# A two-layer Gated DeltaNet and GLA trunk: the scheduler orders the same instructions by its timeline simulation

## The chip, the core and the metric

The kernel runs on 1 core of a Trainium2 chip. The metric is device time in microseconds (us) of one execution, the median of several runs. The engines are PE (TensorE, with PEld its weight loads), DVE (VectorE), ACT (ScalarE), POOL (GpSimd) and SP (SyncE, which only issues DMAs here). Each engine takes its instructions from a queue of its own in the order that the built program gives it, and waits on semaphores for work of the others.

## The reference

One sequence of 2048 tokens with 1024 channels, float32, through two layers. Layer 0 mixes tokens by a gated delta rule (8 heads, keys of 128, values of 256), layer 1 by gated linear attention (GLA, 4 heads). Each layer ends in an output projection, a residual and a layer norm.

```python
def gdn_mixer(x, w_in, conv_w, a_log, dt_bias, norm_w, w_out):
    p = x @ w_in
    qkv = causal_conv_silu(p[..., :GDN_QKV], conv_w)
    ...
    beta = jax.nn.sigmoid(b_logit)
    g = -jnp.exp(a_log) * jax.nn.softplus(a_logit + dt_bias)
    o = gated_delta_rule(q, k, v, g, beta)   # q, k l2-normalised per head
    o = gated_rmsnorm(o, norm_w, gate)
    return o.reshape(B, T, GDN_VAL) @ w_out
...
    # gated_delta_rule, per chunk: (A + I) is unit lower triangular
    uw = triangular_solve(A + eye, rhs)
    def step(S, inp):
        v_new = u_n - w_n @ S
        o = qd_n @ S + qk_n @ v_new
        S = S * gl_n + kd_n.T @ v_new
...
def reference(x, ...):
    for i in range(DEPTH):       # 2: gdn_mixer, then gla_mixer
        x = layer_norm(DEEP_ALPHA * x + mixer(x), ln_g[i], ln_b[i])
```

## The kernel before, in words

The tokens are cut into 4 groups of 512, each of 4 chunks of 128. A *unit* is one head of one layer on one group: 32 DeltaNet units and 16 GLA units, 48 in all. PHASES sets the order of the groups: (layer 0, group 0), (0, 1), (1, 0), (0, 2), (1, 1), (0, 3), (1, 2), (1, 3), with all heads of a group one after the other.

Projections are done in float32r with high and low parts, three matmuls for each product (`mm3`, tiles `xh`, `xl`, `wc`); the recurrences are in float32. Four Python generators write the program (`plan.run`, line 931):

- `gemms` (line 432) writes the input projections of a unit: key and query (`kq`), value (`vt`) and gate (`sg`). They use 3 PSUM buffers `psg`. Weight tiles `wc` are streamed by SP through 16 buffers.
- `preps` (758), by `gdn_prep` (574): transposes of keys and queries, the masked products of keys and queries (`psc<-kq`), and the inverse of the unit triangular matrix of each chunk. For the 16x16 blocks on its diagonal, DVE masks the product (tile `W2`) and reduces it to `X`; ACT's queue issues a DMA of `X` to DRAM (`blk`), SP's queue one that reads it back repeated over partitions (`Arep`); then DVE does 15 steps of two small operations each, `Xt` and `X`. After that come matmuls with `U`, `W2` and `Tm`.
- `chains` (823), by `gdn_chain` (785): the recurrence over the 4 chunks of a unit. PE multiplies the state by the keys (`psh<-S,kq`), DVE makes `Rt`, PE multiplies it by the inverse (`psh<-Rt,D1`, where the inverse `Uf` has taken the tile `D1`), ACT copies the result to `wt`, PE does `psh<-wt,kd`, and DVE updates the state `S`. Beside it `psc<-S,qd` and `psc<-wt,D2` give the output, which DVE gates into `og`. `psh` has one buffer: the next use of it has to wait for DVE's update of `S`, the next head's first one too. At the end of the unit `og` is transposed (`psc<-cst,og`) and split into `oth` (ACT) and `otl` (DVE); the norm factor `z` is computed from `ms` by small DVE operations.
- `outs` (856): the output projection of the unit before, 8 blocks of 6 matmuls (`pso<-wo,oth` and `pso<-wo,otl`, one PSUM buffer), each added to the residual `y` by DVE.

```python
        for q in range(15, 0, -1):                                      # gdn_prep
            v.tensor_tensor(xt[:, :, :q], R[:, q, :, :q], X[:, :, q:q + 1].broadcast_to([P, NC, q]), ALU.mult)
            v.tensor_tensor(X[:, :, :q], X[:, :, :q], xt[:, :, :q], ALU.subtract)
...
            mm(d, p["kd"][:, n], wt[:])                                 # gdn_chain
            v.scalar_tensor_tensor(S[:], S[:], eg[:, 1, u.h, n:n + 1], d, ALU.mult, ALU.add)
```

A small planner in the kernel (`Plan`) keeps a rough clock with a cost for each operation. Each generator yields the time at which its next matmul could have its inputs, and the planner goes on with one that is due, so the four streams are interleaved as they are written. All operations pass through one helper, `Planned`, so every row of the profile has line 121, and rows are told apart by the names of tiles. The framework (`tile.TileContext`) then sets the final order of each engine's queue, allots the buffers and puts in the semaphores. Before the change its scheduler does that in its default way.

## Time and profile before

| | before |
|---|---|
| time, median of 3 runs | 3249.08 us (3248.84 to 3249.32) |
| the profiled execution | 3242.97 us |
| its span, first to last instruction | 3241.1 us |
| mean granted TensorE clock | 0.978 |
| busy: PE, PEld, DVE, ACT, POOL | 95%, 80%, 68%, 36%, 12% |
| DMA | 551.93 MB, mean 170 GB/s |

The profiled execution is one run of its own; its span is what the rows of the trace add up to. In rows of the timeline a row has the start in us from the span's start, the duration in us, the engine, the line, the operation with its tiles (out<-in), the shape, a count where equal instructions follow each other, and in brackets the idle time of the engine before it with what ended that. An fp32 matmul shows as two records. Buffer numbers are left out of the names there (`D` is D1 or D2, `S` the state of any head).

### The profile page before, as it was taken

What the parts mean: (1) busy time and instruction counts of PE and PEld (TensorE: products, weight loads), DVE (VectorE), ACT (ScalarE), POOL (GpSimd) and SP (SyncE); (2) the same over time, 40 slices, a digit from 0 to 9 for tenths busy, and PEclk for the clock granted to TensorE, in tenths of its full rate; (3) what the DMA queues carried; (4) which work ended last, traced back from release to release, by engine and by line L of the source; (5) the groups of instructions that cost most, each with busy time, mean ns of one, the idle gap of its engine ahead of it and who ended that gap; (6) DMA issues with size and microseconds to landing.
All of it is one profiled execution on the core that took longest, in us unless ns stands there. A gap on an engine that the chain in (4) does not pass through costs nothing. (4 is left out here: it accounts for less than half of the span.)

```text
span 3241.1 us, 52660 instructions
## 1 busy us (share of the span) xinstructions
PE 3064.3 (95%) x18430; PEld 2608.5 (80%) x18430; DVE 2192.7 (68%) x6201; ACT 1182.7 (36%) x3091; POOL 395.3 (12%) x642
## 2 busy tenths in 40 slices
PE   8889999998999998999999999999999999999997
PEld 6677777777887887887888788888787888888895
DVE  5776677686666757667767665756876665755677
ACT  4444443332232445433332334423332223343331
POOL 4422321020000223200100000100100000000011
PEclk9999999999999999999999999999999999999998
DMA  7876655464444556755544453655644445465453
GB/s 231 251 225 194 195 168 184 149 215 134 143 141 130 178 174 199 255 183 172 187 149 133 134 168 118 218 179 154 194 141 146 145 143 156 134 211 178 134 166 104
DMA packets 442489, 551.93 MB, mean 170 GB/s; under 512 B 37568, under 2 KB 381888, under 8 KB 430192
## 3 DMA queue, kind: packets, MB, share of 16 engines
q1 hardware_dynamic: 412656, 505.57, 50.3%
q10 hardware_dynamic: 29568, 43.00, 4.0%
q8 instruction: 145, 2.38, 0.3%
q14 instruction: 120, 0.98, 0.1%
HBM read 421.24 MB, written 127.21 MB: 169 GB/s over the span
## 5 line engine op out<-in xcount | busy, mean ns | idle before, releaser
L121 PE MATMUL psg<-xh,wc 128*128 128x512 f32 x2560 | 892.7, 408 | 6.2 <-ACT wc L121 3.2
L121 PE MATMUL psg<-wc,xh 128*128 128x256 f32 (+1 forms) x4096 | 795.8, 291 | 10.1 <-DVE sg L121 3.6
L121 PEld LDWEIGHTS psg<-wc,xh 128*128 128x128 f32 x4096 | 657.7, 191 | 38.9 <-DVE sg L121 4.0
L121 PEld LDWEIGHTS psg<-xh,wc 128*128 128x128 f32 x2560 | 488.8, 192 | 118.4 <-ACT wc L121 4.8
L121 PE MATMUL psg<-wc,xl 128*128 128x256 f32 (+1 forms) x2048 | 582.5, 285 | 0.0
L121 PE MATMUL pso<-wo,oth 128*128 128x512 f32 x1472 | 514.4, 427 | 30.4 <-DVE y L121 27.2
L121 PE MATMUL psg<-xl,wc 128*128 128x512 f32 x1280 | 519.5, 406 | 0.5 <-DVE xl L121 0.5
L121 DVE SCALAR_TENSOR_TENSOR y<-pso,z,y 128x512 f32<-128x512 f32 x368 | 274.4, 746 | 189.6 <-PE pso L121 175.5
L121 PEld LDWEIGHTS psg<-wc,xl 128*128 128x128 f32 x2048 | 391.4, 191 | 1.0
L121 DVE SCALAR_TENSOR_TENSOR acc<-pb,taps,acc 128x512 f32<-128x512 f32 x384 | 300.9, 785 | 116.9 <-ACT acc L121 112.0
L121 PE MATMUL pso<-wo,otl 128*128 128x512 f32 x736 | 303.8, 413 | 54.8 <-DVE otl L121 54.6
L121 PEld LDWEIGHTS pso<-wo,oth 128*128 128x128 f32 x1472 | 255.8, 191 | 80.2 <-DVE y L121 39.9
L121 PEld LDWEIGHTS psg<-xl,wc 128*128 128x128 f32 x1280 | 245.3, 192 | 54.0 <-DVE xl L121 2.0
L121 POOL TENSOR_TENSOR wc<-wraw,wc 128x256 fp32r<-128x256 f32 (+1 forms) x288 | 234.8, 830 | 377.0 <-ACT wc L121 357.4
L121 ACT ACTIVATE junk<-psc 128x128 bf16<-128x128 f32 (+1 forms) x448 | 144.1, 322 | 220.2 <-PE psc L121 185.4
L121 PEld LDWEIGHTS pso<-wo,otl 128*128 128x128 f32 x736 | 140.9, 191 | 94.6 <-DVE otl L121 63.8
L121 ACT ACTIVATE th<-psg 128x256 f32<-128x256 f32 (+1 forms) x256 | 110.0, 435 | 287.5 <-PE psg L121 281.1
L121 DVE TENSOR_TENSOR Xt<-Arep,X 128x60 f32<-128x60 f32 (+14 forms) x480 | 102.5, 214 | 137.2 <-DMA Arep<-blk 123.5
L121 POOL TENSOR_TENSOR y<-y,woraw 128x512 f32<-128x512 f32 x62 | 90.6, 1474 | 735.5 <-DVE y L121 578.9
L121 ACT ACTIVATE D<-D 128x512 f32<-128x512 f32 x160 | 100.0, 631 | 207.3 <-DVE D L121 169.8
L121 ACT COPY pb<-psg 128x512 f32<-128x512 f32 x128 | 74.9, 585 | 272.6 <-PE psg L121 261.6
L121 ACT CAST wc<-wraw 128x256 fp32r<-128x256 f32 (+1 forms) x288 | 113.1, 405 | 163.4 <-DMA wraw<-in_w_in 57.6
(182 smaller groups left out, 4433.0 us busy)
## 6 DMA issues: line engine op xcount, KB each, us to landing
wc<-wk SPq DMA_DIRECT2D x816, 256.0 KB
wk<-wc SPq DMA_DIRECT2D x272, 256.0 KB
wraw<-in_w_in SPq DMA_DIRECT2D x288, 128.0 KB
wo<-k_in_w_out SPq DMA_DIRECT2D x27, 1024.0 KB
wo<-_in_w_out SPq DMA_DIRECT2D x22, 1024.0 KB
wo<-ok_in_w_out SPq DMA_DIRECT2D x21, 1024.0 KB
Arep<-blk SPq DMA_DIRECT2D x32, 512.0 KB
wc<-wk SPq DMA_DIRECT2D x48, 272.0 KB
```

The source lines that it names most:

```text
L121: ins = op(*args, **kw)
```

## The change

`TileContext` gets one argument: its scheduler orders the instructions by a simulated timeline of its own in place of its default order. The kernel's functions, the planner, tiles, buffers and the number of instructions that do work are the same: 15921 matmuls, 6201 DVE, 2730 ACT and 642 POOL operations, and 1820 DMAs on SP and 120 on ACT. What changes is the order on every engine, mostly by some tens of us inside a unit.

```diff
-    with tile.TileContext(nc) as tc:
+    with tile.TileContext(nc, schedule_with_timeline_sim=True) as tc:
```

Three places show it, all in the second group of layer 0 where the recurrence goes from head 4 to head 5; `S_4_...` is the state of head 4, `S_5_...` that of head 5. The preparation there is that of head 5, and `kq_10726` and `acc_10941` belong to head 6.

DVE before, from the last state update of head 4 (the row of `S_4`) on:

```order
L121 SCALAR_TENSOR_TENSOR D_2485_11153<-Gb_11151,gc_7007,cst_63 128x128 x4
L121 SCALAR_TENSOR_TENSOR S_4_15_77<-S_4_15_77,eg_7012,psh_10641 128x256
L121 SCALAR_TENSOR_TENSOR D_2486_11154<-Gb_11151,gc_7007,cst_63 128x128 x3
L121 TENSOR_TENSOR og_10478<-psc_10699,sg_9612 128x256
L121 SCALAR_TENSOR_TENSOR ms_10707<-ms_10707,ssq_10479 128x4
L121 SCALAR_TENSOR_TENSOR D_2486_11154<-Gb_11151,gc_7007,cst_63 128x128
```

Eight small rows of `ms`, `z` and `ztmp` follow, and then, still on DVE before, the first `Xt` with the two splits `otl`:

```order
L121 TENSOR_TENSOR Xt_10658<-Arep_10655,X_10657 128x4x15
L121 SCALAR_TENSOR_TENSOR z_10708<-ztmp_10709,z_10708 128x4
L121 TENSOR_TENSOR otl_10740<-psc_10725,oth_10739 128x512
L121 TENSOR_TENSOR X_10657<-X_10657,Xt_10658 128x4x15
L121 TENSOR_TENSOR ztmp_10709<-z_10708 128x4
L121 TENSOR_TENSOR otl_10749<-psc_10743,oth_10748 128x512
```

DVE after, from the reduction `X` of head 5 on:

```order
L121 TENSOR_REDUCE X_10650<-W_2397_10649 128x64
L121 TENSOR_TENSOR og_10478<-psc_10629,sg_9612 128x256
L121 SCALAR_TENSOR_TENSOR Rt_10694<-psh_10641,s_2241_9883,vt_9393 128x256
L121 SCALAR_TENSOR_TENSOR kq_10726<-th_10811,acc_10806 128x512
L121 SCALAR_TENSOR_TENSOR kq_10726<-th_10843,acc_10838 128x512
L121 SCALAR_TENSOR_TENSOR D_2485_11153<-Gb_11151,gc_7007,cst_63 128x128 x4
L121 SCALAR_TENSOR_TENSOR acc_10941<-pb_10937,taps_65,acc_10941 128x512 x2
L121 TENSOR_TENSOR Xt_10658<-Arep_10655,X_10657 128x4x15
L121 SCALAR_TENSOR_TENSOR acc_10941<-pb_10937,taps_65,acc_10941 128x512
L121 TENSOR_TENSOR X_10657<-X_10657,Xt_10658 128x4x15
L121 SCALAR_TENSOR_TENSOR S_4_15_77<-S_4_15_77,eg_7012,psh_10641 128x256
```

The update of `S_4`, `D_2486`, `og` and all of `ms` and `z` have moved from ahead of the first `Xt` to behind it, and `kq` and `acc` of the head after have moved ahead of it. Behind these rows come, in this order, `Xt`, four rows `D_2486`, `X`, `og`, `ms`, `Rt` of the next head, `Xt`, two `sg`, `ms`, `X`, `qd` and the first `otl`.

PE before, one chunk of the recurrence of head 4, with gemm rows (`psg`) between its steps:

```order
L121 MATMUL psh_10613<-S_4_15_77,kq_9392 128x256
L121 MATMUL psc_10629<-S_4_15_77,qd_9832 128x256
L121 MATMUL psc_10625<-kq_10059 128x256 x2
L121 MATMUL psh_10613<-Rt_10615,D_2221_9819 128x256
L121 MATMUL psg_10728<-xh_6048,wc_10204 128x512
L121 MATMUL psg_10728<-xl_6049,wc_10204 128x512
L121 MATMUL psg_10728<-xh_6048,wc_10204 128x512
L121 MATMUL psh_10613<-wt_10627,kd_9837 128x256
L121 MATMUL psc_10629<-wt_10627,D_2222_9820 128x256
```

PE after, the same chunk and the next:

```order
L121 MATMUL psh_10613<-S_4_15_77,kq_9392 128x256
L121 MATMUL psc_10629<-S_4_15_77,qd_9832 128x256
L121 MATMUL psc_10625<-kq_10059 128x256 x2
L121 MATMUL psh_10613<-Rt_10615,D_2221_9819 128x256
L121 MATMUL psh_10613<-wt_10627,kd_9837 128x256
L121 MATMUL psc_10629<-wt_10627,D_2222_9820 128x256
L121 MATMUL psh_10641<-S_4_15_77,kq_9392 128x256
L121 MATMUL psc_10699<-S_4_15_77,qd_9832 128x256
L121 MATMUL psc_10725<-cst_63,og_10478 128x128 x3
L121 MATMUL psc_10743<-cst_63,og_10478 128x128 x3
L121 MATMUL psh_10641<-Rt_10694,D_2221_9819 128x256
```

The gemm rows have left the chunk. Behind the last row come 22 gate matmuls (`psg<-wc,xh` and `psg<-wc,xl`, 128x256), and then PE after goes on so:

```order
L121 MATMUL psh_10641<-wt_10697,kd_9837 128x256
L121 MATMUL psc_10699<-wt_10697,D_2222_9820 128x256
L121 MATMUL psg_11010<-wc_10832,xh_6184 128x256
L121 MATMUL psg_11010<-wc_10832,xl_6185 128x256
L121 MATMUL psh_11147<-S_5_16_78,kq_10059 128x256
L121 MATMUL psc_10725<-cst_63,og_10478 128x128
L121 MATMUL psc_10743<-cst_63,og_10478 128x128
```

The first `psh` matmul of head 5, which before stands 182 rows behind the last `psc<-wt,D` row of head 4, stands three rows behind it now. On SP, `Arep` stands directly behind a `wo` load (in the first group its `woraw` loads) in both orders; the `wc` loads have moved with their gemms.

## The prediction

> **What bounds the kernel now.** I read the page first (its spans, shares and clock), then the list of waits on PE, then the timeline of one place where PE waits long, engine by engine.
>
> ```profile
> span 3241.1 us, 52660 instructions
> PE 3064.3 (95%) x18430; PEld 2608.5 (80%) x18430; DVE 2192.7 (68%) x6201; ACT 1182.7 (36%) x3091; POOL 395.3 (12%) x642
> PEclk9999999999999999999999999999999999999998
> ```
> ```profile
> engine line waited for: us in total, times, longest us
> PE pso L121 <- DVE otl L121: 54.6, 18, 6.4
> PE pso L121 <- DVE y L121: 27.2, 17, 4.4
> PE psh L121 <- DVE S L121: 10.9, 9, 3.2
> PE psh L121 <- ACT wt L121: 9.9, 7, 2.7
> PE psc L121 <- DVE U L121: 7.3, 3, 5.6
> ```
>
> PE is the bound, busy in 95% of the span, and every matmul is the same after the change. So a new order can only win or lose PE's idle time and what the clock does behind it. The largest wait is for `otl`. The next rows, of DVE, of PE, and of the ACT and SP queues, show where it comes from, in a unit (one head of one token group) of the first group and in one of the second.
>
> ```profile
> 416.26 1.01 DVE L121 TENSOR_REDUCE X<-W 128x64 f32<-128x512 f32 x1
> 421.76 0.17 DVE L121 TENSOR_SCALAR ms<-ms 128x4 f32<-128x4 f32 x1
> 428.83 0.22 DVE L121 TENSOR_TENSOR Xt<-Arep,X 128x60 f32<-128x60 f32 x1 [6.90 <-DMA Arep<-blk]
> 428.97 0.16 DVE L121 TENSOR_SCALAR z<-ms 128x4 int32<-128x4 int32 x1
> 430.05 0.69 DVE L121 TENSOR_TENSOR otl<-psc,oth 128x512 fp32r<-128x512 f32 x1
> ```
> ```profile
> 430.79 0.80 PE L121 MATMUL pso<-wo,otl 128*128 128x512 f32 x1 [5.73 <-DVE otl L121]
> ```
> ```profile
> 978.66 0.61 DVE L121 SCALAR_TENSOR_TENSOR D<-psc,br,D 128x128 f32<-128x128 f32 x2
> 980.65 1.03 DVE L121 TENSOR_REDUCE X<-W 128x64 f32<-128x512 f32 x1
> 981.71 0.33 ACTq L121 DMA_DIRECT2D blk<-X  x1
> 983.24 0.63 SPq L121 DMA_DIRECT2D Arep<-blk  x1
> 984.36 0.48 DVE L121 SCALAR_TENSOR_TENSOR S<-S,eg,psh 128x256 f32<-128x256 f32 x1
> 990.28 0.22 DVE L121 TENSOR_TENSOR Xt<-Arep,X 128x60 f32<-128x60 f32 x1 [2.48 <-DMA Arep<-blk]
> ```
>
> DVE reduces the 16x16 blocks into `X`, two DMAs carry them through DRAM and back (`blk`, `Arep`), and DVE's first `Xt` waits for the second. From the end of `X` to `Xt` it is 428.83 - 417.27 = 11.6 us in the first group and 990.28 - 981.68 = 8.6 us later. What stands behind `Xt` on DVE waits with it though it doesn't need it: `z<-ms` was ready at 421.93 and ran at 428.97. Today PE is first held by `otl`; the state update `S` was already done (984.36).
>
> **The change.** Nothing is added or removed; the rows are permuted. The order of after, as shown above, moves two things that matter. On DVE the update `S` of a head's last chunk now stands three rows behind the first `Xt`. On PE the next head's first `psh` matmul, which needs that update since `psh` is one buffer, now stands close behind the chain. In 22 of the 32 DeltaNet units the order has this; in 4 more, the last heads of a group, the first row held is `pso<-wo,otl`.
>
> *The new wait, per unit.* PE's rows between the last `psc<-kq` and the held `psh` are, by the order, 8 fp32 matmuls of 256 columns, 6 transposes and 24 gate matmuls. Their pace:
>
> ```profile
> 981.17 0.59 PE L121 MATMUL psh<-S,kq 128*128 128x256 f32 x2
> 981.60 0.59 PE L121 MATMUL psc<-S,qd 128*128 128x256 f32 x2
> 982.03 0.49 PE L121 MATMUL psc<-cst,og 128*128 128x128 f32 x3
> 982.46 0.70 PE L121 MATMUL psh<-Rt,D 128*128 128x256 f32 x2
> 983.62 0.70 PE L121 MATMUL psh<-wt,kd 128*128 128x256 f32 x2
> ```
> ```profile
> 451.41 0.40 PE L121 MATMUL psg<-wc,xh 128*128 128x256 f32 x2
> 451.65 0.28 PE L121 MATMUL psg<-wc,xl 128*128 128x256 f32 x1
> 451.76 0.39 PE L121 MATMUL psg<-wc,xh 128*128 128x256 f32 x2
> ```
> ```profile
> L121 DVE SCALAR_TENSOR_TENSOR acc<-pb,taps,acc 128x512 f32<-128x512 f32 x384 | 300.9, 785 | 116.9 <-ACT acc L121 112.0 <-ACT gc L121 0.5
> L121 DVE SCALAR_TENSOR_TENSOR D<-Gb,gc,cst 128x128 f32<-128x128 f32 x256 | 79.8, 354 | 14.7 <-PE psh L121 8.6 <-DMA Gb<-gcT 5.7
> L121 DVE SCALAR_TENSOR_TENSOR sg<-th,psg 128x256 f32<-128x256 f32 x192 | 79.4, 415 | 111.4 <-ACT th L121 90.4 <-ACT ba L121 20.1
> L121 DVE SCALAR_TENSOR_TENSOR kq<-th,acc 128x512 f32<-128x512 f32 x64 | 45.0, 703 | 6.6 <-ACT th L121 5.6
> ```
>
> 981.60 - 981.17 gives 0.43 us for an fp32 matmul, about 0.11 a transpose, and 0.35 us for three gate matmuls: 8 x 0.43 + 6 x 0.11 + 24 x 0.117 = 6.9 us of PE work. DVE needs 3.0 us from the first `D` to the end of `X` (978.66 to 981.68), then 8.6 for the round trip, then Xt 0.22, acc 0.79, X 0.21 and S 0.48 = 1.7: in all 13.3 us. PE idles 13.3 - 6.9 = 6.4 us, and 9.4 with the 11.6 of the first group, which has 6 of the 22 units. The 4 last heads have 8.4 us of PE work against 3.0 + 8.6 + 1.1: 4.3 us. Sum: 6 x 9.4 + 16 x 6.4 + 4 x 4.3 = **+176**. Ends: all at 8.6 us, 158; the later groups up to 2 us longer, since their first heads wait longer in the DVE row below, 210.
>
> ```profile
> DVE Xt L121 <- DMA Arep<-blk: 123.5, 31, 7.5
> ```
>
> *What goes.* The 54.6 us for `otl`, which this wait replaces, and a part of the 27.2 for `y`, some of which stand behind the same `Xt`: **-65**, ends -55 and -82.
>
> *What is late next.* DVE comes out of the wait with a backlog. By the order, Xt, four D (4 x 0.35), X and `og` (0.42) stand between `S` and the next transposes, 2.2 us, and PE has one matmul of 0.43: 1.7 us of wait. Then ms, Rt, Xt and `sg` (0.42) before a gate matmul that needs a free psg: another 1.0. 2.7 x 22 = **+60**, ends 35 and 90.
>
> *The recurrent chain.* From `psh<-Rt` to `psh<-wt` the rows above need 983.62 - 982.46 = 1.16 us (two passes, ACT's copy `wt`, the next start). Before, gemm rows lay between; after, nothing in most chunks, so PE has 0.43 and waits 0.7. From `psh<-wt` to the next `psh<-S,kq` it is 0.70 + 0.48 + some 0.1 = 1.3, with 0.86 of work: 0.4. Chunks 2 and 3 lie inside the wait above and cost nothing more; chunks 0 and 1 of 32 units cost 2 x 1.1 x 32 = 70, against 10.9 + 9.9 today: **+50**, ends 40 and 70.
>
> *The clock.* In the rows of stretches here and below the columns are the stretch, its length, busy us of PE, PEld, DVE, ACT and POOL (with instructions), the granted clock, the DMA engines' busy share and GB/s.
>
> ```profile
> 428.50:435.30 6.80, 4.51 (x11) 3.55 (x12) 5.96 (x31) 1.10 (x3) 0.90 (x3) 0.50 0.21 72
> 991.60:995.10 3.50, 3.50 (x10) 2.72 (x9) 2.79 (x14) 0.00 (x0) 0.00 (x0) 0.51 0.01 2
> ```
>
> Behind the 5.73 us wait PE has clock 0.50 for 6.8 us, behind the 2.53 us one for 3.5. So 18 stretches of 3.4 to 6.8 us go, worth half of that (about 40 us), and 26 of 6.8 come, worth 88; but DVE's backlog holds PE for 2.7 of them anyway, and work at half speed fills that. I take **0**, ends -40 and +45. The Trainium skill ("TensorE: Matmul & The Clock Gate", HAM oscillation) asks for no idle gaps over about 3.4 us. By that rule the 2.53 us gap would have cost no clock; the trace has it at 0.51, so by the rule the -40 would be about -20, and the total 20 us more.
>
> *The GLA units.* The order gives DVE less lead over PE in each group's first GLA unit. Nothing in the trace shows it; I bound it by none and by one wait of the longest for `S` (3.2) in each of 16 units, 51, and take **+20**, nearer to none as few units change.
>
> *Queues.* On SP, `Arep` still stands directly behind the unit's `wo` load, and the weight tiles move with their gemms. I cost that at 0: the whole unit of 66.5 us below has DMA engines busy 0.46, which covers a shift of some tens of us; if that cover is gone, psg matmuls wait for `wc`. POOL moves with them, busy 2.35 of 66.5 us there.
>
> ```profile
> 924.00:990.50 66.50, 63.66 (x376) 53.23 (x376) 44.56 (x133) 20.12 (x59) 2.35 (x9) 1.00 0.46 140
> ```
>
> Sum: 176 - 65 + 60 + 50 + 0 + 20 = +241. The profiled execution took 3242.97 us (span 3241.1 and 1.9 around it), 6 under the median 3249.08 of the three timed runs. Forecast: 3249 + 241 = **3490 us**, 7.4% slower.
>
> **Rivals.**
> - *The round trip is covered.* Between `X` and `Xt` the new order gives DVE og 0.42, Rt 0.48, two kq 1.4, four D 1.4 and two acc 1.6: 5.3 us. If `blk` and `Arep` together took no more (the first leg takes 1.5, 981.71 to 983.24), the hold shrinks to 3.0 + 5.3 + 1.7 - 6.9 = 3.1 in 22 units and 1.0 in 4: 72, and the time is 3249 + 72 - 65 + 60 + 50 + 20 = 3386. Against it: the second leg took 7.0 at a time when the queue was quiet. The Trainium skill ("DMA: Bandwidth & Descriptors", Anatomy of one DMA) gives about 2.0 us fixed plus bytes at 436 GB/s, an estimate of 2 x 2.0 + 1.2 = 5.2 us for both, so by that page this rival would hold; the trace has 8.6 and 11.6.
> - *Faster: S isn't held.* If DVE got to `S` without waiting for `Arep`, no later than 2.2 us after `X` (6.9 - 3.0 - 1.7), PE would find its rows ready, the 176 and 60 fall away, and the gaps and their slow clock go: -65 - 40 + 50 + 20 = -35, 3214 us. For it: `S` doesn't need `Xt`. Against: `z<-ms` at 428.97, which didn't either and waited.
> - *The backlog spreads.* DVE stays late through the GLA units too: a wait of the size of the longest for `U`, 5.6 us, in each of 16, 90 in place of 20: 3560 us. For it: DVE is busy 44.56 of 66.5 us in that unit and loses 6 more to `Arep`.
> - *No effect.* The rows move by tens of us inside a unit and the total stays. Against: it would need the new wait to equal what goes.
>
> **How the numbers follow.** The forecast as it stands 0.69, covered round trip 0.09, spread backlog 0.16, S not held 0.04, no effect 0.02. The low ends of all terms give 158 - 82 + 35 + 40 - 40 + 0 = +111, 3360; the high ends 210 - 55 + 90 + 70 + 45 + 51 = +411, 3660. They won't all fall together: 3370 to 3600 takes in the covered round trip and the spread backlog and leaves out under 2 in 10. Two runs of one kernel differ by under 0.02% here, but 0.2% is about what can be told from no change: faster 0.04, same 0.02, slower 0.94.
>
> **What would show it.** In the profile after: a row PE psh <- DVE S of about 100 to 200 us in some 22 long waits, in place of `otl`; `Xt` waiting for `Arep` in most units as now, with 8 to 12 us from `X`; PE psh <- ACT wt of tens of us in waits of about 0.7; PE's share near 90% and units of the second group near 75 us instead of 66.5. Wrong would make me: a round trip under 5 us, a wait for `S` that is small because other waits have already delayed PE before it, or waits for `wc` on PE.

## The result, and the profile after

| | before | after |
|---|---|---|
| time, median of 4 runs | 3248.96 us (3244.58 to 3249.32) | 3458.01 us (3453.57 to 3461.16) |
| the profiled execution | 3242.97 us | 3461.16 us |
| its span | 3241.1 us | 3459.4 us |
| granted TensorE clock | 0.978 | 0.962 |

The ratio is 1.0646, with a 95% interval of 1.0627 to 1.0664: 6.5% slower; the medians differ by 209 us. The forecast was 3490 us in a range of 3370 to 3600. The medians of the kernel before in the comparisons below differ by some us (3243 to 3251), so each experiment is given with its ratio to the runs of before beside it. Of the page of the kernel after, the span, the busy time of PE and the clock in 40 slices:

```profile
span 3459.4 us, 52624 instructions
PE 3154.0 (91%) x18430; PEld 2650.5 (77%) x18430; DVE 2183.3 (63%) x6201; ACT 1178.9 (34%) x3091; POOL 390.1 (11%) x642
PEclk9999999999999999999999999999999999999998
```

PE's idle time is span less busy: 3459.4 - 3154.0 = 305.4 us, where before it was 3241.1 - 3064.3 = 176.8. So 129 us of the loss are new idle time. The other 90 us are in PE's busy time (3154.0 - 3064.3), for the same matmuls. About two thirds of that is the clock: 3459.4 x (1 - 0.962) = 131 us lost to it against 3241.1 x (1 - 0.978) = 71 before, 60 more. That counts idle time at half clock too; by PE's busy time at half clock alone (212.7 us against 104.4, of which half is lost) it is 54. The other 30 to 36 are matmul rows that got longer at full clock. The list of waits on PE tells who makes it idle (it names the releaser, the total in us, how often, the longest):

```profile
PE psh L121 <- DVE S L121: 91.0, 39, 4.5
PE psh L121 <- ACT wt L121: 40.2, 78, 2.3
PE psc L121 <- DVE og L121: 24.0, 31, 2.7
PE pso L121 <- DVE y L121: 18.5, 21, 4.3
PE psh L121 <- DVE Rt L121: 15.4, 10, 3.8
PE psg L121 <- DVE sg L121: 15.3, 31, 2.2
PE psg L121 <- ACT acc L121: 15.2, 25, 0.7
...
PE pso L121 <- DVE otl L121: 2.9, 4, 1.1
```

The wait for `otl`, 54.6 us before, is gone, and the wait for `S` heads the list in its place. Of the gaps between PE's matmuls ahead of `psh`, 25 are of 3.19 us or more. In 22 of them the first `psh` row of a head waits for `S` (3.26 to 4.54 us, 83 us in sum); in the other 3, in last heads of a group, PE waits for `Rt`. The place that the order showed (head 4 to head 5, second group), in the timeline of DVE and then of PE:

```profile
924.84 0.61 DVE L121 SCALAR_TENSOR_TENSOR D<-psc,br,D 128x128 f32<-128x128 f32 x2 [0.81 <-PE psc L121]
...
926.83 1.01 DVE L121 TENSOR_REDUCE X<-W 128x64 f32<-128x512 f32 x1
...
936.21 0.22 DVE L121 TENSOR_TENSOR Xt<-Arep,X 128x60 f32<-128x60 f32 x1 [3.95 <-DMA Arep<-blk]
...
937.14 0.48 DVE L121 SCALAR_TENSOR_TENSOR S<-S,eg,psh 128x256 f32<-128x256 f32 x1
...
938.84 0.42 DVE L121 TENSOR_TENSOR og<-psc,sg 128x256 f32<-128x256 f32 x1
```
```profile
932.64 0.59 PE L121 MATMUL psh<-wt,kd 128*128 128x256 f32 x2
...
937.67 0.70 PE L121 MATMUL psh<-S,kq 128*128 128x256 f32 x2 [3.77 <-DVE S L121]
939.31 0.69 PE L121 MATMUL psc<-cst,og 128*128 128x128 f32 x2 [0.94 <-DVE og L121]
```

`Xt` starts 936.21 - 927.84 = 8.4 us after the end of `X`, having waited 3.95 of them with nothing else to do. `S`, whose input from PE was ready at about 933.2, runs behind it, PE gets its `psh` row at 937.67, and `og` comes later still. The Trainium skill ("PSUM — Partial Sum Buffer", Engine vs sequencer instructions) says that VectorE's queue is strictly first in, first out, and that matmuls start in program order; the trace agrees, with `S` held from 933.2 to 937.14 behind a row it doesn't need. DVE's wait for `Arep` is as large as before (123.5):

```profile
DVE Xt L121 <- DMA Arep<-blk: 122.7, 31, 7.8
```

Behind the wait the clock is low, and a unit has grown to 75.1 us from 66.5 (stretches as in the prediction; the granted clock is the number behind POOL's):

```profile
937.70:944.50 6.80, 5.64 (x24) 4.83 (x25) 6.29 (x29) 2.39 (x5) 0.00 (x0) 0.54 0.27 64
933.90:1009.00 75.10, 67.60 (x377) 55.37 (x376) 43.06 (x130) 20.05 (x60) 1.92 (x9) 0.95 0.40 124
```

### The profile page after: what moved, and what is told of

It is laid out like the page before. It is cut to its first block, busy times and chain, and to the rows that moved or that the text cites. A ratio compares the mean times of both kernels' runs of the same rounds, so it can differ in the third digit from the quotient of the medians.

```text
span 3459.4 us, 52624 instructions
## 1 busy us (share of the span) xinstructions
PE 3154.0 (91%) x18430; PEld 2650.5 (77%) x18430; DVE 2183.3 (63%) x6201; ACT 1178.9 (34%) x3091; POOL 390.1 (11%) x642
## 5 line engine op out<-in xcount | busy, mean ns | idle before, releaser
L121 PE MATMUL psg<-wc,xh 128*128 128x256 f32 (+1 forms) x4096 | 846.9, 301 | 35.6 <-ACT acc L121 15.2
L121 PE MATMUL psg<-xh,wc 128*128 128x512 f32 x2560 | 839.0, 401 | 14.7 <-ACT wc L121 9.0
L121 PEld LDWEIGHTS psg<-wc,xh 128*128 128x128 f32 x4096 | 689.5, 201 | 81.5 <-ACT acc L121 25.2
L121 PE MATMUL psg<-wc,xl 128*128 128x256 f32 (+1 forms) x2048 | 602.2, 296 | 0.2 <-DVE xl L121 0.2
L121 PEld LDWEIGHTS psg<-xh,wc 128*128 128x128 f32 x2560 | 483.5, 189 | 126.4 <-ACT wc L121 11.6
L121 PE MATMUL psg<-xl,wc 128*128 128x512 f32 x1280 | 509.5, 398 | 0.0
L121 PE MATMUL pso<-wo,oth 128*128 128x512 f32 x1472 | 485.5, 411 | 19.1 <-DVE y L121 18.5
L121 PEld LDWEIGHTS psg<-wc,xl 128*128 128x128 f32 x2048 | 407.9, 200 | 7.9 <-DVE xl L121 0.4
L121 PE MATMUL pso<-wo,otl 128*128 128x512 f32 x736 | 294.6, 400 | 2.9 <-DVE otl L121 2.9
L121 PE MATMUL psh<-S,kq 128*128 128x256 f32 x256 | 94.9, 455 | 101.0 <-DVE S L121 90.8
```

Source lines behind the costliest of these rows:

```text
L121: ins = op(*args, **kw)
```

## The experiments

The theory is the prediction's: what PE needs next (`S`, then `og`, then `otl`) stands on DVE behind the `Xt` that waits for a round trip through DRAM, and the recurrence on PE is packed so densely that each step's latency shows. The rivals: the packing alone, the other engines' order alone, the clock, the round trip as such. All edits use the same device, an ordering edge that makes one instruction stand behind another on the same engine and adds no semaphore. What an edge doesn't hold the scheduler may still move, so each run is the cost of its edit with the order that came of it:

```diff
+    def behind(later, earlier):
+        tc.add_manual_dep(later.ins, earlier.ins.name, mybir.DependencyInfo(
+            mybir.DependencyClass.NoSync, mybir.DependencyReason.DATA))
```

### e1: only S ahead of Xt

In the kernel after, the loop of `Xt` begins behind the last `S` of the head before (a head's prep first lets the planner write that far).

```diff
+        if not u.first:
+            yield from after(("S", u.at - 1))
         for q in range(15, 0, -1):
-            v.tensor_tensor(xt[:, :, :q], ...
+            ins = v.tensor_tensor(xt[:, :, :q], ...
+            if q == 15 and not u.first:
+                behind(ins, row["S", u.at - 1])
```

> The kernel after, with one constraint: the first Xt of a head stands on DVE behind the last state update S of the head before it (S is 1 row ahead of Xt instead of 3 behind); og and otl stay behind Xt, the round trip and the dense chain stay. Theory hold (what costs is everything PE's next rows need that is queued on DVE behind the Xt that waits for Arep): psh<-S no longer waits, but the next PE row but one, psc<-cst,og, waits for og behind the same Xt, so the hold moves there; gain only about 22 x 1.3 us (two matmul groups of 0.6 to 0.7 us more before PE stops) = 29 us, 3430 us (3400 to 3450), and the half-clock pieces stay. Rival S alone (only the row that PE was seen waiting for matters): the 91.0 us of psh<-S waits and the half clock behind them go, 3320 us or less. Rival dense chain or queue order: nothing moves, 3450 to 3465.

Measured: 3423.08 us, ratio 1.0537 (1.0514 to 1.0559). 35 us are won, about what the theory gave. Two rows of the waits on PE:

```profile
PE psc L121 <- DVE og L121: 85.4, 32, 4.4
...
PE psh L121 <- DVE S L121: 10.1, 26, 1.3
```

The wait for `S` has fallen from 91.0 to 10.1 us, and that for `og`, which PE's very next row needs, has risen from 24.0 to 85.4. The row on which PE was seen waiting isn't the cause; the next one behind the same `Xt` takes its place. S alone as the cause is refuted.

### e2: S, og and otl ahead of Xt

The same edit with the second `otl` in place of `S`:

```diff
+        if not u.first:
+            yield from after(("oT", u.at - 1))
...
+            if q == 15 and not u.first:
+                behind(ins, row["otl", u.at - 1])
```

> The kernel after, with one constraint: the first Xt of a head stands on DVE behind the second otl of the head before it, so S, og and otl are all ahead of the Xt that waits for Arep. PE's order stays that of the kernel after (7 rows between the chunks of the recurrence, 35 to the next head). Theory hold: the waits psh<-S (91.0), psc<-og (24.0) and most of psg<-sg (15.3) go, and with them the half-clock pieces of some 2 us in 22 units: 3458 - 91 - 20 - 10 - 40 = about 3300 us (3230 to 3340); the rest over the kernel before is the dense chain. Rival dense chain (the recurrence packed on PE is what costs): only the direct waits turn into chain waits, 3400 us or more. Rival late prep: Xt, now later, makes the next head's Uf late, and PE waits there instead: 3440 us or more, with new waits psc<-U or psh<-Rt.

Measured: 3338.52 us, ratio 1.0279 (1.0256 to 1.0302). 120 us are won, so the hold with what followed it cost 3.7% of the time before; late prep is refuted. The time lies at the upper edge of what was expected, and 2.8% over before remain, with the recurrence on PE packed as in the kernel after (7 rows between the later chunks of a head, 35 from the last one to the next head; of PE's other rows the matmuls of the inverse move most, by some 15 records, to a later place). PE's waits, and the span with its clock:

```profile
PE psh L121 <- ACT wt L121: 46.2, 84, 1.9
PE psc L121 <- DVE og L121: 25.6, 33, 2.8
...
PE psh L121 <- DVE S L121: 12.2, 21, 2.9
```
```profile
core 0: 3336.1 us, clock 0.984
```

What remains is seen in the timeline of PE in one unit, where a whole chunk of the recurrence runs with nothing between its steps but two `psc<-kq` of the prep:

```profile
881.77 0.70 PE L121 MATMUL psh<-S,kq 128*128 128x256 f32 x2
882.31 0.59 PE L121 MATMUL psc<-S,qd 128*128 128x256 f32 x2
882.74 1.03 PE L121 MATMUL psc<-kq 128*128 128x256 f32 x4
883.61 0.59 PE L121 MATMUL psh<-Rt,D 128*128 128x256 f32 x2
884.66 0.70 PE L121 MATMUL psh<-wt,kd 128*128 128x256 f32 x2 [0.46 <-ACT wt L121]
885.20 0.59 PE L121 MATMUL psc<-wt,D 128*128 128x256 f32 x2
885.93 0.70 PE L121 MATMUL psh<-S,kq 128*128 128x256 f32 x2
```

From one chunk to the next it is 885.93 - 881.77 = 4.16 us for 7 matmuls of 0.43, 3.01 us of work. Of the 1.15 us lost the list of waits names 0.46; the rest lies in rows that start late or run longer behind a wait (0.70 in place of 0.59). Whoever adds up named waits alone misses more than half of what a packed chain costs.

### e3: no round trip

In the kernel after, `Arep` is read from a block written once at the start; `X` still goes out to `blk`. Both transfers stay, and what the kernel leaves out is that the second needs the first: its inverse is of another block, and its output is not the reference's.

```diff
             sync.dma_start(R[:].rearrange("p s n j -> p (s n j)"),
-                            bc(blk[:].rearrange("(b s) n -> b (s n)", b=8), 1, 16))
+                            bc(blk0[:].rearrange("(b s) n -> b (s n)", b=8), 1, 16))
```

> The kernel after with Arep loaded from a block written once at the start instead of from this head's blk (the write of blk stays, and so do all transfers by number and size); the inverse is then of wrong blocks. The scheduler keeps S behind the first Xt (7 rows) and PE's order in the first two groups. Theory hold: Xt no longer waits (122.7 us of DVE's wait for Arep go to under 20), so S behind it holds nobody: psh<-S falls from 91.0 to about 15 us, og and sg with it, and the half clock behind: 3458 - 76 - 20 - 10 - 40 = about 3310 us (3240 to 3350). Rival order alone (S behind 15 rows of DVE work is enough, or the dense chain is what costs): 3400 us or more with PE's waits where they were.

Measured: 3311.62 us, ratio 1.0193 (1.0172 to 1.0214): 146 us won, with `S` still behind `Xt`. PE's wait for `S`:

```profile
PE psh L121 <- DVE S L121: 11.2, 24, 1.5
```

`Xt` has no row of waiting for `Arep` any more. Taking away what makes `Xt` wait does at least as much (146 us) as taking the held rows out from behind it (120), so the hold is shown from both sides.

### e4: the kernel before, with otl ahead of Xt

The edit of e2 in the kernel before, with the default scheduler.

> The kernel before (default scheduler) with the first Xt of a head behind the second otl of the head before it on DVE. Theory hold: in the kernel before it is otl that stands behind Xt in second groups, and its 54.6 us of PE waits (pso<-otl) are the same hold in a milder form; they go, and a part of the clock lost behind them: 3249 - 55 - 20 = about 3175 us (3140 to 3210), faster than both. Rival late prep: Xt is later by up to 8 us, the next head's Uf comes late, 3249 us or more. Rival slack: otl's wait is replaced by the wait y or by chain waits: 3220 to 3250.

Measured: 3167.84 us, ratio 0.9748 (0.9728 to 0.9767), faster than both kernels. Rows of PE's waits:

```profile
PE pso L121 <- DVE y L121: 26.1, 22, 3.6
PE psg L121 <- DVE sg L121: 14.4, 7, 4.2
...
PE psh L121 <- DVE S L121: 13.1, 9, 3.2
...
PE pso L121 <- DVE otl L121: 0.9, 3, 0.5
```

The 54.6 us for `otl` are gone, and the clock has risen to 0.988: 3168.3 x 0.012 = 38 us lost to it, against 71. The kernel before had the hold too, in a milder form. The edit moves rows of PE as well (the matmuls of the inverse by some 38 records), but the two terms, 54 and 33 us, cover the 79 us won.

### e8: S held where PE doesn't need it

In the kernel before, the last `S` of a head is put directly behind the first `Xt` of the next head; on PE 180 of 18430 records move, and no `psh` row.

```diff
+            update = lambda n=n, d=d: v.scalar_tensor_tensor(S[:], ...
...
+                ins = update()               # the last S of a head
+                if n == NC - 1 and ("Xt", u.at + 1) in row:
+                    behind(ins, row["Xt", u.at + 1])
```

> The kernel before, with the last state update S of a head put on DVE directly behind the next head's first Xt (in before it stands 10 to 15 rows ahead of it), so S waits for Arep as in the kernel after; nothing else is asked, and PE's order is the same row for row: the next psh<-S stands some 180 rows later. Theory hold (a held S costs only where PE has the row that needs it close by): 0 to 15 us more, 3247 to 3262. Rival hold as such (S behind a waiting Xt costs wherever PE stands): 22 x 4 us = 90 us more, 3335 us or more. Rival gain (an update out of the way of og and the otl path): under 3240 us.

Measured: 3238.81 us, ratio 0.9992 (0.9979 to 1.0006): no difference. The timeline of one unit, of DVE and then PE's next row of `psh<-S`, and PE's whole wait for `S`:

```profile
988.76 0.22 DVE L121 TENSOR_TENSOR Xt<-Arep,X 128x60 f32<-128x60 f32 x1 [2.32 <-DMA Arep<-blk]
988.90 0.47 DVE L121 SCALAR_TENSOR_TENSOR S<-S,eg,psh 128x256 f32<-128x256 f32 x1
```
```profile
1029.71 0.70 PE L121 MATMUL psh<-S,kq 128*128 128x256 f32 x2
```
```profile
PE psh L121 <- DVE S L121: 12.0, 11, 3.2
```

`S` is held behind `Xt` as in the kernel after, and PE comes for it 40 us later. So `S` behind `Xt` on DVE costs nothing until `psh` has moved up close on PE.

### e5, e6, e7: PE in the order in which the program writes it

To see what the rest is, e5 holds every matmul of the kernel after in the order in which the planner writes it, e6 does so on top of e2, and e7 does it on top of e2 for the recurrence's matmuls against all other PE rows.

```diff
             ins = op(*args, **kw)
+            if self.key in "t":              # TensorE
+                if self.last is not None:
+                    PIN[0].add_manual_dep(ins.ins, self.last.ins.name, ...NoSync...)
+                self.last = ins
```

> The kernel after, with every TensorE instruction held in the order in which the program's planner writes it; DVE, ACT, POOL and the queues are still ordered by the simulation. PE's chunks of the recurrence then stand 25, 5 and 15 rows apart and the next head's first one 275 rows on (after: 7, 7, 35, 271), and the last S of a head lands 16 rows ahead of the next Xt. Theory PE order (the loss came through PE's rows standing close behind what feeds them, the hold and the packed chain both): the 209 us go, 3215 us (3170 to 3265). Rival other engines (the simulated order of DVE, ACT and the DMA queues costs by itself): 60 us or more of the loss stay, 3310 us or more. Rival hold alone (only the hold went with e2): 3338 us, as e2.

> e2 and e5 together: the simulated order, PE in the order of the program, and the first Xt of a head behind the second otl of the head before it. Theory PE order: as the kernel before with otl ahead (e4, 3168 us), since neither hold nor packed chain is left: 3170 us (3145 to 3205). Rival other engines: the 170 us between e2 and e4 are not PE's order but that of the other engines, and half of it or more stays, 3250 us or more.

> e2 (otl ahead), with only the five matmuls of each chunk of the DeltaNet recurrence kept where the program's planner writes them among PE's other rows (22, 8 and 9 rows between chunks instead of 7, 7 and 35); all other PE rows, the linear-attention layer's too, stay as the simulation orders them. It splits the 170 us between e2 (3338) and e4 (3168). Theory chain (the packed recurrence is the larger part, by the waits psh<-wt 46.2, psc<-og 25.6, psh<-Rt 5.8 of e2, some 78 us, with the half clock behind): 3245 us (3215 to 3275). Rival other rows (gate matmuls right behind the sg and acc that free their banks, GLA, output): 50 us or less go, 3290 us or more.

Measured: 3396.92 us (1.0481, 1.0466 to 1.0497), 3392.36 us (1.0465, 1.0450 to 1.0481) and 3377.76 us (1.0415, 1.0400 to 1.0431). All three missed the theory by 130 to 220 us and lie where the rivals put them (other engines in e5 and e6, other rows in e7); e6 and e7 are slower than e2. The first two rows of PE's waits in e5, and two of e7:

```profile
PE psh L125 <- DVE Rt L125: 62.0, 57, 2.0
PE psh L125 <- DVE S L125: 49.0, 39, 4.7
```
```profile
PE psh L124 <- ACT wt L124: 57.9, 105, 2.1
PE psc L124 <- ACT W L124: 33.8, 58, 3.2
```

The mistake was to take the planner's order for that of the kernel before. It is a third order, packed in its own way (in the first group the chunks of e5 stand 25, 5 and 15 rows apart, those of before 26, 13 and 10), so these runs left the question open. e9 below has the simulated order around PE's order of before and is 69 us faster than e5, so the default scheduler's rearranging of the planner's rows was part of what made the kernel before fast.

### e9, e10, e11: one engine in the other kernel's order

The names of the instructions are the same in both kernels, so an engine can be held row by row in the order of the other: e9 gives the kernel after the PE order of before, e10 its DVE order, and e11 gives the kernel before the PE order of after. All other engines are ordered by the respective scheduler around that.

```diff
+            if self.key == "t":              # "v" in e10
+                ALL[ins.ins.name] = ins
...
+    at, last = 0, None
+    for step in struct.unpack(f"<{len(d) // 4}i", d):    # d: the other kernel's row names, as steps
+        at += step
+        ins = ALL[f"I-{at}"]
+        if last is not None:
+            behind(ins, last)
+        last = ins
```

> The kernel after, with the 15921 matmuls held in exactly the order that they have in the kernel before; DVE, ACT, POOL and the queues are ordered by the simulation around them (on DVE S then stands 8 rows ahead of the first Xt and otl 18 and 21 behind). It mends e5: the planner's order of e5 is not the order of before. Theory PE order: the change costs through PE's rows alone, so the time is that of before, 3245 us (3220 to 3285); otl, which PE needs next in before's order, is held as in before or somewhat longer. Rival other engines: the simulated order of DVE, ACT and queues keeps 60 us or more of the loss, 3305 us or more.

> The kernel after, with DVE's 6201 instructions held in the order of the kernel before; PE, ACT, POOL and the queues are ordered by the simulation around them. On DVE the last S stands 10 rows ahead of the first Xt and otl 10 and 13 behind; on PE the chunks stand some 7 to 17 rows apart and 60 to the next head. Theory hold plus packed PE: S holds nobody, PE stays packed behind og, wt and acc, otl is held as in before: 3330 us (3280 to 3390). Rival DVE order (with DVE's order back, the loss goes): 3270 us or less. Rival no part (DVE's order is not where it comes from): 3440 us or more.

> The kernel before (default scheduler), with the matmuls held in exactly the order that they have in the kernel after; DVE, ACT, POOL and the queues are ordered by the default scheduler around them. On DVE the last S then stands 1 row ahead of the first Xt, og and otl behind it, as in e1. Theory PE order: the loss comes with PE's rows, as in e1: 3425 us (3390 to 3465). Rival other engines: 3300 us or less.

Measured: e9 3328.19 us, 1.0253 (1.0236 to 1.0270); e10 3723.06 us, 1.1472 (1.1449 to 1.1496); e11 3432.82 us, 1.0570 (1.0554 to 1.0585). PE's waits in e9, then in e11:

```profile
PE pso L177 <- DVE otl L177: 70.0, 21, 6.3
PE psh L177 <- DVE S L177: 32.1, 28, 4.3
```
```profile
PE psc L206 <- DVE og L206: 59.0, 30, 3.6
PE psg L206 <- DVE sg L206: 39.9, 14, 11.3
PE psh L206 <- ACT wt L206: 38.8, 77, 2.0
```

e11 came out as expected: PE's order alone, brought into the kernel before, costs 5.7% of the 6.5, with `og` held and the chain packed as in e1. e9 missed: with PE's order of before the simulation puts `otl` 18 and 21 rows behind `Xt` in the first group (before: 10 and 13), the hold on `otl` is longer than before (70.0 against 54.6), and 2.5% stay, which is in the range of the rival, the other engines. e10 missed the theory by 393 us; its time is in the open range of the rival "no part" (3440 us or more), but that rival had no reason for a time so far above the kernel after. Its largest waits on PE and on DVE:

```profile
PE pso L185 <- DVE y L185: 143.2, 73, 9.4
```
```profile
DVE S L185 <- PE psh L185: 422.9, 90, 17.9
```

DVE waits for PE's recurrence and PE for DVE's `y`: as far as these waits tell, DVE's order, fixed from another schedule, and a newly simulated one of PE don't fit. Two engines' orders are a pair, so "the loss of one engine's order" is no fixed number: PE's order costs 5.7% when it is brought in (e11), gives back 3.9 of the 6.5 points when it is taken out (e9), and swapping DVE's alone costs more than twice the whole loss.

### e12: e4's PE order and otl ahead, the rest simulated

The edit of e2, and PE's rows held in the order of e4.

> The kernel after with both: the first Xt of a head behind the second otl of the head before it (e2), and the matmuls held in exactly the order that they have in e4; the other engines and the queues are ordered by the simulation around them. It asks what the 80 us are that e9 kept over the kernel before, where PE waited 70.0 for otl and 32.1 for S. Theory hold (in e9 the simulation put otl 18 and 21 rows behind Xt in place of 10 and 13, so the hold grew): it is gone here, the time is near e4's 3168, 3190 us (3155 to 3220), and PE waits for otl under 10 and for S under 20 us. Rival other engines (the simulated order of ACT and the queues costs 80 us by itself): 3235 us or more, with PE's waits at other names.

Measured: 3227.35 us, ratio 0.9927 (0.9906 to 0.9948), just between the two. Rows of PE's waits:

```profile
PE psh L176 <- DVE S L176: 28.9, 24, 4.3
...
PE pso L176 <- DVE otl L176: 0.7, 2, 0.4
```

The wait for `otl` that e9 had is gone, as the theory said, and the time fell by 3.3% from e9's (whose PE order is that of before, a little different from e4's). But 1.8% over e4 remain, under the same PE order and with `Xt` two to four rows behind `otl` in both; `S` is 28.9 us against 13.1 in e4. What in the simulated order of the other engines makes it so wasn't separated further.

With e4, e12, e2 and after in a row, each differing from the one ahead in one edit, the loss falls into steps (of the time of before): the hold on `otl` taken out of before, -2.5%; the other engines' simulated order, +1.8%; PE's simulated order with no hold, +3.5%; the hold in that order, +3.7%. On 3249 us that is -82, +58, +114 and +119. They are sizes of edits: with PE's rows set free in the third step, the other engines' rows move too.

## Why the prediction was right, point by point

The direction, the mechanism and the range held; 3490 was 32 us too high. The terms agree less well than the sum.

- *PE is the bound and only its idle time and clock can move.* Right, with an addition: 30 to 36 us went into rows that run longer at full clock. No term named them; that of the chain, taken from elapsed times, holds a part.
- *The new wait, +176.* The place, the mechanism (e2, e3, e8) and the number were right: 22 units forecast with a long wait for `S`, 22 seen. The elapsed time was right too: from the start of `D` (924.84) to the end of `S` 12.8 us against 13.3. The term was mis-sized, since the row shows 91.0 us, 83 of them in those 22 waits. First, the round trip of the first group was put at 11.6 us; in the kernel after it was 7.9 to 8.8 us in heads 1 to 7 of it, which makes the 9.4 of six units about 6.2 and takes 19 us. It came with less traffic: before, two loads of `woraw` are issued 1.1 us ahead of the `Arep` at 419.11, and the DMA engines are busy 0.82 of the time from `X` to `Xt` (417.27 to 428.83); after, the loads of that head are issued 13 us ahead, and the share is 0.27 (464.13 to 472.01). That this shortened it wasn't tried. Second, between the last `psc<-kq` and the `psh` at 937.67 PE's rows took 7.9 us, not 6.9, and of the 5.0 us idle (6.4 forecast) only 3.77 are under the name of `S`; 1.2 are waits for `wt` (0.46), `acc` (0.62) and shorter gaps, which the term had counted as its own. Third, the 17 us for `otl` in 4 more units came to 2.9 at most. In their place stand three waits for `Rt` that no term had, 10 us in sum, and there `Rt` stands on DVE behind rows of a GLA unit's preparation, not behind an `Xt`.
- *What goes, -65.* `otl` from 54.6 to 2.9 and `y` from 27.2 to 18.5: -60.
- *What is late next, +60.* `og` 24.0, `sg` 15.3 and `acc` from ACT 15.2; the list of before had 1.6 for `og`, 4.9 for `sg` and no row for `acc` from ACT. That is +33 for the two that the term had, and +15 for `acc`, which it didn't have. e1 showed how these stand in line.
- *The recurrent chain, +50.* `wt` and `Rt` 55.6 against 9.9 for `wt` and 0.5 for `Rt`: +45 in named waits, and the 1.1 us a chunk were 1.15 in e2. What the term had not said is that two more chunks of a unit can cost this once the hold is gone; the 46.2 us for `wt` in e2, where 3338 us remain, fit that, but it wasn't tried apart.
- *The clock, 0.* This step was wrong: +54 to +60 us, beyond its own upper end of +45. What failed is the overlap, "work at half speed fills that". In the stretch shown PE works 5.64 of 6.80 us at half clock, which loses some 2.8, and is idle 1.16, for `og` and `sg`, in place of 2.7. So half clock does fill some of the backlog's wait, but at most the 27 us that `og` and `sg` came in under their term, not the 48 (88 less 40) that it was put at. By the Trainium skill ("TensorE: Matmul & The Clock Gate", HAM oscillation) gaps over about 3.4 us lose the clock; all 25 long waits have half clock starting within 1.7 us of their end (0.54 in the stretch shown), so the trace agrees for the 21 over 3.4 us, but the other 4, of 3.19 to 3.27, lost it too. What decides in this trace is told below.
- *The GLA units, +20.* From the first `psh` row of a run of GLA units to its last, 226.3, 211.9 and 401.8 us before and 247.7, 226.6 and 390.8 after: +25 in sum.
- *Queues, 0.* PE's waits for `wc` from ACT are 10.5 us after, against 6.4 in the list of before: +4.

The terms of the new wait, of what is late next and of the chain add up to 176 + 60 + 50 = 286; the list of named waits shows 173 more for `S`, `wt`, `Rt`, `og`, `sg` and `acc`. The clock was forecast at 0 and is, with the longer rows, 90. That 3490 came within 32 us is in good part luck: two errors opposed each other.

Of the rivals, the covered round trip is refuted: it takes 7.9 us or more in every unit, where the estimate by the Trainium skill ("DMA: Bandwidth & Descriptors", Anatomy of one DMA, a fit of DMAs that GpSimd issues) was 5.2; these are issued by ACT and SP. With an `Xt` that doesn't wait for it (e3) the time is 3312. "S isn't held" fell with the result, and e1 showed that this alone would have won 35 us. The backlog did not spread: the GLA units took 25 us more, not 90.

## What to carry to other kernels

On an engine that takes its rows in order, whatever another engine needs soon should stand ahead of the row that waits for a DMA; ordering edges of one kind, one for each head, took 2.5% off the kernel before (e4). A held row costs nothing by itself (e8); it costs when its consumer on the other engine has been moved up close, so read a new order as pairs of engines, and when the waiting row is mended ask which row behind the same wait PE comes to next (e1). When the bound is one engine, price a new order by idle time, clock and longer rows together, from span, busy time and clock, and take the list of named waits for the places, not for the sum.

## What the hardware showed that was not expected

What sets the clock back is how long PE idles within some 3.4 us, in one wait or in several. In each trace all stretches of half clock start on one grid of 3.413 us, and apart from the tail those of the kernel after last 3.41 us (14 times), 6.83 (26) or 10.24 (2); no other length occurs. Cut into the windows of its grid, the traces of before, after and e2 together have 2786 windows at full clock, and behind 87 of them comes half clock. If PE is idle for more than 1.8 us of a window, half clock follows, and if less, full clock, in all but 9 of the 2786 (those 9 have 1.25 to 1.85 us idle). Half clock stays for one more window when PE idles 0.59 us or more in a window of it, and ends when PE idles 0.54 or less; there is no exception in the three.

So a single wait shorter than a window can be enough, and where it falls on the grid matters: in the trace of before all 8 gaps of 3.5 us or more between matmuls have half clock behind them, of the 28 between 1.5 and 3.5 us 18 have, and of 48 of 0.3 to 1.5 us none. Short waits add up when they fall close together: 4 of the 19 stretches of e2 have no gap of 1.5 us in the 3.4 us ahead of them, but two shorter ones. Spread thin they cost less clock: e2 has PE busy 3100.8 us of 3336.1, 235 us idle, more than the 177 of the kernel before; yet its clock is 0.984 against 0.978, 53 us lost against 71, with 60 us of its idle time in gaps of 1.5 us or more where before has 112.

Behind each of the 22 long waits for `S` half clock lasts 6.83 us, since PE idles on in its first window (at the place shown 1.16 us, for `og` and `sg`). So such a wait of some 4 us costs PE up to 3.4 us more behind it.
